# A later due time for the residual's transposes, an own due time for a projection's second half, and bias tables stored in 16 parts

## The chip, the cores and the metric

The kernel runs on one core of a Trainium2 chip. The metric is the device time of one execution in microseconds (us). TensorE is called PE, VectorE DVE, ScalarE ACT, GpSimd POOL; SP is the engine whose queue issues every DMA here.

## The reference, cut to what matters

Four layers work on a [256, 1024] float32 array. Each layer is: a half-step SwiGLU feed-forward (1024 to 2 x 2816 to 1024), a token mixer, and a second half-step feed-forward. Each of these three sub-layers has an RMS norm before and after it, and its normed output is added to the residual x.

```python
for i in range(4):
    g = norm_g[i]
    x = x + 0.5 * rms_norm(swiglu(rms_norm(x, g[0]), ffn_w_in[i, 0], ffn_w_out[i, 0]), g[1])
    m = mixer[i % 3](rms_norm(x, g[2]))       # 0: sliding window, 1: sparse, 2: block
    x = x + rms_norm(m, g[3])
    x = x + 0.5 * rms_norm(swiglu(rms_norm(x, g[4]), ffn_w_in[i, 1], ffn_w_out[i, 1]), g[5])
```

All mixers have 16 heads of 64 and add a bias to their scores that depends on the distance of query and key and on the head. Two tables hold it: table 1 with the 128-wide band for layers 0 and 3, table 0 for layers 1 and 2.

## The kernel before, in words

**Two chains.** The 256 rows are two tiles of 128, and each tile is a chain (`Chain(0)`, `Chain(1)`) that goes through all layers. A chain is a Python generator: it emits a piece of work and then yields the time at which its next piece can start. Chain 0 leads by up to a few weight slabs (`LEADS`). Weights are streamed once: SP loads half slabs of 128 x 1024 float32 into four `raw` buffers, ACT rounds each to `hi`, DVE subtracts to `lo`, and both chains multiply by both parts. An activation is also held as `xh` and `xl`, so a product takes three matmuls: hi by xh, lo by xh, hi by xl. The slots for `hi` and `lo` (28 in the pool `p4`) are shared with the tables and the mixers' arrays; `room()` counts them.

**The rough clock.** The order of PE's instructions is written out by the generators: PE runs in program order (`ORDERED`), and the framework orders the other engines. The order comes from a rough clock in the kernel's builder. `Clock.book` gives each ACT, DVE, POOL and DMA instruction a rough time, `when(tile)` says when a tile will have been written by that clock, and each yield carries such a time. `choose` takes of all generators the one whose time is earliest (not before now), and on a tie the one with the lower rank: the setup first, then chain 0, then chain 1. A yield whose second member is True also waits until the next weight slab has been split. None of this exists on the chip: a wrong rough time shows up as PE waiting in order for something late, while other work stands behind it.

**What runs at a boundary.** At the end of each sub-layer `boundary` takes the sum of squares of the accumulator (ACT), multiplies by the gain (DVE, `k<-acc,g`), takes the reciprocal root (POOL, `r`) and adds to the residual in two halves (DVE, `x<-k,r,x`). Then it yields `when(x_)`, and next it emits eight PE transposes of x (`trx`), from which ACT makes `xh` and DVE makes `xl`. There are 24 boundaries, of which the last two end the kernel without transposes.

**A projection.** `project(512)` in the mixers emits 12 matmuls over the first four blocks of 128 inputs, yields, and emits 12 over the last four. The feed-forward does the same in `ffn`, and there the second half has its own time, `when(self.xl[4])`. In `project` the yield carries 0.0: due at once.

**The mixers' core.** `core` does four heads at a time: scores on PE (`acc<-k,k`), bias on DVE (`k<-acc,bias`), exponent on ACT, transposes of the probabilities on PE (`trp`), copied by ACT and DVE (`pT`), and the product with the values (`pv`). `trq` are transposes of queries and keys. Bias tiles are read from a DRAM array `scratch` by four DMAs each.

**The setup.** It starts once, early in layer 0, with the lowest rank. It makes the two bias tables (PE `tab`, DVE copies to `rows`), then writes each to `scratch` with 32 copies: two DMAs of 16 copies for table 1 and two for table 0, with `SGAP` us of the rough clock after each. Only after the last does it give back two slots of the pool (`drop(3, 2)`).

Of the kernel before, what the change touches and what calls it, by code (L numbers as in the profile page):

```python
# [22 lines left out]
H = 16  # L23
# [10 lines left out]
LT = 384  # L34
GELU_C = 0.7978845608028654

REP = 32
# [6 lines left out]
PACE = 1.2  # L44
LATE = 6
SETUP = 30
SGAP = 8
SOON = 3
HALVES = (slice(0, DH), slice(DH, P))
FIRST, CMP_CORE = -1, 1.5  # L50
# [97 lines left out]
class Clock:  # L148
# [8 lines left out]
    def when(self, *tiles):  # L157
        return max(self.written.get(tile_of(a), 0.0) for a in tiles) + self.LAG

    def free(self, *tiles):  # L160
        return max(self.read.get(tile_of(a), 0.0) for a in tiles) + self.LAG
# [20 lines left out]
def tile_of(a):  # L182
    return getattr(a, "tensor", a).name
# [77 lines left out]
def trunk(ctx: ExitStack, tc: tile.TileContext, x, rel, gains, pre, sinks, pos, w1, w2, wts, hot,  # L261
          cmask, bmask, out, scratch):
    clock = Clock()
    when, free = clock.when, clock.free
    nc = Engines(tc.nc, clock)
# [34 lines left out]
    def k4(who, shape, dtype=F32):  # L300
        plan.held[who] += 1
        assert sum(plan.held) + 2 * (plan.split - plan.freed) <= SLOTS
        return p4.tile(shape, dtype, tag="k4", name="k4")

    def drop(who, n=1):
        plan.held[who] -= n

    def k2(shape, dtype=F32):
        return p2.tile(shape, dtype, tag="k2", name="k2")

    def bank(shape, name):
        p = mm_ps.tile(shape, F32, tag="mm", name=name)
        banks.append(p)
        if len(banks) > 4:
            clock.read[tile_of(p)] = free(banks.pop(0))
        return p

    def free_bank():
        return free(banks[0]) if len(banks) == 4 else 0.0
# [14 lines left out]
    def setup():  # L334
        relx = const.tile([33, 2, H], F32, name="relx")
        hots = k4(3, [P, HALF])[:33, :2 * LT]
        nc.sync.dma_start(relx[0:32], rel)
        nc.vector.memset(relx[32:33], 1.0)
        nc.sync.dma_start(hots, hot)
        nc.sync.dma_start(cm, cmask)  # L340
        nc.sync.dma_start(bm, bmask)
        nc.sync.dma_start(post, pos)
        nc.sync.dma_start(w2s, w2)
        for a in range(2):
            nc.sync.dma_start(nsink[:, a, :], sinks[a:a + 1, :].broadcast_to([P, H]))
        yield when(hots, relx), False
        rows = k4(3, [P, HALF])[:H, :2 * LT].rearrange("p (a b) -> p a b", a=2)
        for i in range(2):
            p = bank([P, 512], "tab")
            nc.tensor.matmul(p[:H, :LT], relx[:, i, :], hots[:, i * LT:(i + 1) * LT],  # L350
                             start=True, stop=True)
            nc.vector.tensor_copy(rows[:, i, :], p[:H, :LT])
        nc.vector.tensor_scalar_mul(nsink, nsink, -1.0)
        for i in (1, 0):
            for c in range(0, REP, REP // 2):
                nc.sync.dma_start(scratch[i, :, c:c + REP // 2],
                                  rows[:, i, :].unsqueeze(1).broadcast_to([H, REP // 2, LT]))
                yield clock.now + SGAP, False
        drop(3, 2)
        plan.want[3] = 0  # L360
# [44 lines left out]
    def load_gains(*keys):  # L405

        for i, k in keys:
            if i < DEPTH and k < 6:
                g = pg.tile([P, D], F32, tag="g", name="g")
                nc.sync.dma_start(g, gains[i, k:k + 1, :].broadcast_to([P, D]))  # L410
                gains_on[i, k] = g

    class Chain:
# [72 lines left out]
        def boundary(self, acc, this, coef, last=False):  # L486


            t = self.t
            x_ = xt[t]  # L490
            g = self.gain(*this)
            cols = [slice(q * 512, (q + 1) * 512) for q in range(2)]
            r = self.rsqrt(self.var(acc, 1.0 / (coef * coef)))
            ys = []
            for c, a in zip(cols, acc):
                y = k2([P, 512])
                nc.vector.tensor_tensor(y, a, g[:, c], op=ALU.mult)
                ys.append(y)
            accs.extend(acc)
            for c, y in zip(cols, ys):  # L500
                nc.vector.scalar_tensor_tensor(x_[:, c], y, r, x_[:, c], op0=ALU.mult, op1=ALU.add)
                if last:
                    nc.sync.dma_start(out[t * P:(t + 1) * P, c], x_[:, c])
            if last:
                return
            yield max(when(x_), free_bank()), False
            i, k = this
            norm = 6 * i + k + 1
            self.split_T(x_, 0, norm)
            self.split_T(x_, 1, norm)  # L510
            self.v = self.var([x_[:, c] for c in cols], 1.0)
            if t:
                load_gains(((norm + 1) // 6, (norm + 1) % 6))
            yield when(self.xl[0]), True
# [14 lines left out]
        def project(self, n):  # L529
            p = bank([P, 512], "proj")  # L530
            if n > 256:
                self.proj(p, n, 0, 4)
                yield 0.0, True
                self.proj(p, n, 4, 8)
            else:
                self.proj(p, n, 0, 8)
            return p
# [527 lines left out]
    with tc.manual_schedule(engines=ORDERED):  # L1065
        make_identity(tc.nc, ident)
        nc.vector.memset(mhalf, -0.5)
        for c in (slice(0, 512), slice(512, 1024)):
            nc.sync.dma_start(xt[0][:, c], x[:P, c])
        nc.sync.dma_start(pres, pre)  # L1070
        load(2)
        nc.sync.dma_start(xt[1], x[P:, :])
        for t in range(2):
            start(both[t].run(), t, t * LATE)
        n = 0
        while running:
            if n:
                feed(n < 8)
            best = choose()
            while best is None:  # L1080
                assert feed(True)
                best = choose()
            (at, _), one = best
            clock.now = max(at, clock.now)
            n += 1
            if n == SETUP:
                start(setup(), FIRST)
            got = next(one[1], None)
            if got is None:
                running.remove(one)  # L1090
            else:
                one[2:] = got
            done = min(c.at for c in both)
            plan.freed = last_half[done - 1] if done else 0
# [29 lines left out]
```

## Time and profile before

| | us |
|---|---|
| median of 3 runs | 1977.15 (1976.63 to 1980.09) |
| the profiled execution's own time | 1981.12 |
| its span, first to last instruction | 1979.3 |
| PE busy | 1938.0 (98%) |
| PE weight loads busy | 1586.7 (80%) |
| DVE busy | 1234.2 (62%) |
| ACT busy | 1039.2 (53%) |
| DMA queues, share of 16 engines | 55.7% |
| mean granted PE clock | 0.994 |

A matmul's busy time includes the pipeline, so consecutive matmuls overlap in the records and a busy PE isn't PE at its peak. What tells is the distance from one start to the next: 0.228 us for a product of 128 x 128 with 512 columns where nothing disturbs it.

### The profile page before, as it was taken

How to read it: one execution, taken by the hardware profiler on the slowest of the kernel's cores; microseconds unless marked ns; L12 is line 12 of the kernel's file. 1: busy time of each engine (PE TensorE's matmuls, PEld its weight loads, DVE VectorE, ACT ScalarE, POOL GpSimd, SP SyncE). 2: the span in 40 equal slices, each digit the busy share in tenths (PEclk: the TensorE clock that was granted, in tenths of full speed). 3: DMA queues.
4: the chain of work that ended last, by engine and by line, in shares of the span. 5: the costliest groups of instructions: out<-in, count | busy, mean ns of one | idle time of the engine just before them, and what ended most of it. 6: DMA issues, size and time to landing. Idle time of an engine off the chain costs nothing.

```text
span 1979.3 us, 27414 instructions
## 1 busy us (share of the span) xinstructions
PE 1938.0 (98%) x9978; PEld 1586.7 (80%) x9978; DVE 1234.2 (62%) x2267; ACT 1039.2 (53%) x1885; POOL 43.0 (2%) x62
## 2 busy tenths in 40 slices
PE   7999999999999998999999999999999999999998
PEld 6778878888888876788888888778888888878887
DVE  6566666556655648765576556566557655676554
ACT  6345655445544546554455455655445544665442
POOL 0000000000000000000000000000000000000000
PEclk9999999999999999999999999999999999999999
DMA  8758556555556454465556555655555555436551
GB/s 271 210 192 241 176 137 200 190 185 186 195 188 193 153 165 116 139 202 188 185 170 209 185 185 175 188 148 196 185 189 181 195 188 191 161 112 205 185 186 58
DMA packets 114131, 356.42 MB, mean 180 GB/s; under 512 B 12843, under 2 KB 30507, under 8 KB 113996
## 3 DMA queue, kind: packets, MB, share of 16 engines
q1 hardware_dynamic: 113996, 354.68, 55.4%
q8 instruction: 78, 1.28, 0.3%
q14 instruction: 57, 0.47, 0.1%
HBM read 352.01 MB, written 2.62 MB: 179 GB/s over the span
## 4 chain that ended last, share of the span: by engine, by line
PE 90%; ACT 3%; DVE 3%; DMA 2%; issue 1%; SPq 0%; POOL 0%; DVEq 0%; POOLq 0%; ACTq 0%
PE proj L228 56%; PE acc L228 29%; ACT k L210 2%; PE trh L235 2%; DVE k L210 2%; DMA raw<-wts 1%; PE trx L235 1%; DVE lo L210 1%; PE pv L228 1%; DMA bias<-scratch 1%; PE trp L235 1%; ACT hi L210 1%; DVE pT L210 0%; PE trq L235 0%; ACT xh L210 0%
## 5 line engine op out<-in xcount | busy, mean ns | idle before, releaser
L210 DVE TENSOR_TENSOR lo<-raw,hi 128x1024 fp32r<-128x1024 f32 x625 | 760.3, 1223 | 371.3 <-ACT hi L210 338.7
L210 ACT ACTIVATE hi<-raw 128x1024 fp32r<-128x1024 f32 x625 | 659.3, 1063 | 369.3 <-PE acc L228 187.5
L228 PE MATMUL proj<-hi,xh 128*128 128x512 f32 (+1 forms) x1696 | 673.9, 398 | 2.7 <-DVE xl L210 1.7
L228 PE MATMUL proj<-lo,xh 128*128 128x512 f32 (+1 forms) x1696 | 657.4, 389 | 0.8 <-DVE lo L210 0.8
L228 PE MATMUL proj<-hi,xl 128*128 128x512 f32 (+1 forms) x1696 | 448.6, 387 | 0.0
L228 PEld LDWEIGHTS proj<-hi,xh 128*128 128x128 f32 x1696 | 320.0, 189 | 64.0 <-ACT xh L210 2.8
L228 PEld LDWEIGHTS proj<-lo,xh 128*128 128x128 f32 x1696 | 320.4, 189 | 61.4 <-DVE lo L210 1.1
L228 PEld LDWEIGHTS proj<-hi,xl 128*128 128x128 f32 x1696 | 315.6, 188 | 67.3
L228 PE MATMUL acc<-hi,hh 128*128 128x512 f32 x704 | 223.7, 392 | 3.1 <-ACT hh L210 3.1
L228 PE MATMUL acc<-lo,hh 128*128 128x512 f32 x704 | 222.2, 389 | 0.0
L228 PE MATMUL acc<-hi,hl 128*128 128x512 f32 x704 | 191.3, 390 | 0.0
L210 ACT ACTIVATE h<-proj,rh 128x256 f32<-128x256 f32 x176 | 81.9, 465 | 182.3 <-PE proj L228 180.8
L210 ACT ACTIVATE hh<-trh 128x256 fp32r<-128x256 f32 x176 | 67.0, 380 | 180.8 <-PE trh L235 180.7
L228 PEld LDWEIGHTS acc<-hi,hh 128*128 128x128 f32 x704 | 130.9, 188 | 30.2 <-ACT hh L210 3.9
L228 PEld LDWEIGHTS acc<-hi,hl 128*128 128x128 f32 x704 | 132.1, 188 | 27.7
L228 PEld LDWEIGHTS acc<-lo,hh 128*128 128x128 f32 x704 | 132.1, 188 | 27.6
L210 DVE SCALAR_TENSOR_TENSOR h<-h,proj 128x256 f32<-128x256 f32 x176 | 73.6, 418 | 116.2 <-ACT h L210 116.1
L210 DVE TENSOR_TENSOR hl<-trh,hh 128x256 fp32r<-128x256 f32 x176 | 73.9, 420 | 113.2 <-ACT hh L210 113.1
L210 DVE SCALAR_TENSOR_TENSOR h<-proj,c,h 128x256 f32<-128x256 f32 x176 | 85.0, 483 | 5.1
L210 ACT ACTIVATE k<-k,nm 128x128 f32<-128x128 f32 (+1 forms) x160 | 70.7, 445 | 32.0 <-DVE nm L210 32.0
L210 POOL TENSOR_TENSOR r<-v,mhalf 128x1 f32<-128x1 f32 x48 | 36.0, 750 | 1818.4 <-DVE v L210 1818.4
L235 PE MATMUL trh<-ident,h 128*128 128x128 f32 x352 | 67.0, 272 | 0.0
(99 smaller groups left out, 1133.4 us busy)
## 6 DMA issues: line engine op xcount, KB each, us to landing
raw<-wts SPq DMA_DIRECT2D x624, 512.0 KB, 4.6
bias<-scratch SPq DMA_DIRECT2D x96, 128.0 KB, 4.6
g<-gains SPq DMA_DIRECT2D x12, 512.0 KB, 4.8
k<-w SPq DMA_DIRECT2D x8, 512.0 KB, 8.3
scratch<-k SPq DMA_DIRECT2D x4, 384.0 KB, 6.6
out<-x SPq DMA_DIRECT2D x4, 256.0 KB, 2.0
x<-x SPq DMA_DIRECT2D x2, 256.0 KB, 3.0
x<-x SPq DMA_DIRECT2D x1, 512.0 KB, 7.2
```

Of the source, the lines that this page charges most:

```text
L210: return call(out, *args, **kw)
L228: self.engine.matmul(out, lhs, rhs, **kw)
L235: self.engine.transpose(out, src, ident)
```

## The change

Four edits. `SGAP` goes from 8 to 6. The tables are stored in parts of 4 copies instead of 16: 16 DMAs in place of 4, the same bytes. At a boundary the time that is yielded for the transposes of x is 1.5 us of the rough clock later (`SLACK`). In `project` the second half is due when `xl[4]` is written by the rough clock, no longer at once.

```diff
-SGAP = 8
+SGAP = 6
+SLACK = 1.5
...
         for i in (1, 0):
-            for c in range(0, REP, REP // 2):
-                nc.sync.dma_start(scratch[i, :, c:c + REP // 2],
-                                  rows[:, i, :].unsqueeze(1).broadcast_to([H, REP // 2, LT]))
+            for c in range(0, REP, 4):
+                nc.sync.dma_start(scratch[i, :, c:c + 4],
+                                  rows[:, i, :].unsqueeze(1).broadcast_to([H, 4, LT]))
                 yield clock.now + SGAP, False
...
-            yield max(when(x_), free_bank()), False
+            yield max(when(x_) + SLACK, free_bank()), False
             i, k = this
...
                 self.proj(p, n, 0, 4)
-                yield 0.0, True
+                yield when(self.xl[4]), True
                 self.proj(p, n, 4, 8)
```

## Rows read from the trace of the kernel before

**Rows 1.** The table of busy times by stretch (busy us and count of PE, PE weight loads, DVE, ACT, POOL; then the granted clock, the DMA engines' share and GB/s): a stretch of feed-forward, and three with mixers' cores.

```profile
50.00:75.00 25.00, 25.00 (x113) 20.60 (x114) 15.85 (x21) 11.79 (x15) 0.00 (x0) 1.00 0.67 220
...
750.00:775.00 25.00, 20.27 (x302) 15.74 (x298) 23.10 (x98) 15.73 (x55) 1.56 (x2) 1.00 0.34 96
...
1275.00:1300.00 25.00, 21.89 (x243) 17.44 (x243) 18.99 (x99) 20.26 (x75) 0.00 (x0) 1.00 0.50 139
...
1725.00:1750.00 25.00, 23.21 (x175) 17.45 (x173) 17.57 (x87) 18.59 (x66) 0.00 (x0) 0.86 0.56 158
```

**Rows 2.** The waits of PE over the whole span, longest first: who waited, for whom, us in total, times, the longest.

```profile
PE trx L235 <- DMA x<-x: 8.4, 2, 4.7
...
PE trx L235 <- DVE x L210: 2.4, 2, 2.0
...
PE proj L228 <- DVE xl L210: 1.7, 2, 1.3
```

**Rows 3.** The setup's store and the bias reads: the DMA issues of the span, the instructions on the tile `scratch` and on the tile `bias` (shortest, median and longest duration, first and last start).

```profile
raw<-wts SPq DMA_DIRECT2D x624, 512.0 KB, 4.6
bias<-scratch SPq DMA_DIRECT2D x96, 128.0 KB, 4.6
...
scratch<-k SPq DMA_DIRECT2D x4, 384.0 KB, 6.6
```

```profile
L248 SPq DMA_DIRECT2D bias<-scratch x96: 302/430/1672, 146.6 to 1743.8; - x96
L248 SPq DMA_DIRECT2D scratch<-k x4: 332/384/426, 82.2 to 116.8; - x4
```

```profile
L210 DVE CUSTOM_DVE_ANT_0 k<-acc,bias x160: 254/340/425, 235.6 to 1759.8; 128x128 f32<-128x128 f32 x80, 128x256 f32<-128x256 f32 x80
```

**Rows 4.** The timeline of SP's queue around the first stores (start, us, operation, count), and the load of the DMA engines from 80 to 120 us in 40 slices of 1 us.

```profile
82.21 0.98 SPq L248 DMA_DIRECT2D scratch<-k  x2
84.90 7.72 SPq L248 DMA_DIRECT2D raw<-wts  x4
92.67 0.42 SPq L248 DMA_DIRECT2D scratch<-k  x1
104.95 1.46 SPq L248 DMA_DIRECT2D raw<-wts  x2
```

```profile
DMA  9507888888999899997000000178788961004789
GB/s 258 205 20 98 101 101 100 98 101 110 164 313 197 213 283 410 430 385 177 12 0 0 0 0 0 25 221 246 287 270 315 418 266 49 0 0 160 242 315 361
```

**Rows 5.** The timeline of ACT and of PE at 102 to 106 us.

```profile
102.24 0.47 ACT L210 ACTIVATE h<-proj,rh 128x256 f32<-128x256 f32 x1 [2.37 <-PE proj L228]
102.61 3.89 ACT L210 ACTIVATE hi<-raw 128x1024 fp32r<-128x1024 f32 x4
```

```profile
102.72 0.39 PE L228 MATMUL proj<-lo,xh 128*128 128x512 f32 x1
103.72 0.50 PE L228 MATMUL proj<-hi,xh 128*128 128x512 f32 x1 [0.60 <-ACT hi L210]
104.98 0.50 PE L228 MATMUL proj<-lo,xh 128*128 128x512 f32 x1 [0.76 <-DVE lo L210]
```

**Rows 6.** The timeline of PE at two boundaries of chain 0 at a feed-forward's end, then the transposes `trx` alone in four such boundaries' stretches (at 217.8 that of chain 1, for comparison).

```profile
198.80 1.08 PE L228 MATMUL proj<-hi,xl 128*128 128x512 f32 x4
199.97 1.23 PE L235 MATMUL trx<-ident,x 128*128 128x128 f32 x8
200.96 0.71 PE L228 MATMUL acc<-hi,hh 128*128 128x512 f32 x2
```

```profile
1692.68 1.08 PE L228 MATMUL proj<-hi,xl 128*128 128x512 f32 x4
1693.75 1.23 PE L235 MATMUL trx<-ident,x 128*128 128x128 f32 x8
1694.73 0.48 PE L228 MATMUL acc<-hi,hh 128*128 128x512 f32 x1
```

```profile
217.80:219.20 1.40, 1.03 (x8) 0.81 (x8) 0.00 (x0) 0.66 (x3) 1.00 0.88 325
657.00:658.40 1.40, 1.23 (x8) 0.84 (x8) 0.00 (x0) 0.00 (x0) 1.00 0.77 298
1008.90:1010.30 1.40, 1.23 (x8) 0.84 (x8) 0.00 (x0) 0.00 (x0) 1.00 0.79 281
```

**Rows 7.** The timeline at the end of layer 0's mixer, chain 0's boundary beside the last products of chain 1's core.

```profile
272.71 1.42 DVE L210 SCALAR_TENSOR_TENSOR x<-k,r,x 128x512 f32<-128x512 f32 x2
...
273.61 1.94 PE L235 MATMUL trx<-ident,x 128*128 128x128 f32 x8 [1.98 <-DVE x L210]
...
274.38 0.68 DVE L210 COPY pT<-trp 128x512 f32<-128x512 f32 x1
...
275.48 1.79 PE L228 MATMUL pv<-k,pT 128*64 128x64 f32 x32
...
277.20 0.50 PE L228 MATMUL proj<-hi,xh 128*128 128x512 f32 x1
```

**Rows 8.** Chain 1's boundary at the start of layer 1's mixer: the timeline of PE, then the table by stretch at and after it (columns as in rows 1).

```profile
677.29 1.05 PE L228 MATMUL proj<-hi,xl 128*128 128x48 f32 x8
...
678.18 1.09 PE L235 MATMUL trx<-ident,x 128*128 128x128 f32 x8
...
679.63 0.76 PE L228 MATMUL proj<-hi,xh 128*128 128x512 f32 x1 [0.36 <-ACT xh L210]
```

```profile
679.70:683.12 3.42, 3.42 (x8) 2.71 (x9) 3.07 (x12) 3.42 (x11) 0.35 (x1) 0.50 0.83 266
683.12:686.50 3.38, 3.38 (x16) 2.75 (x15) 3.38 (x5) 1.72 (x2) 0.19 (x1) 1.00 0.48 147
```

**Rows 9.** Chain 1's boundary at the start of layer 2's mixer, timeline.

```profile
1214.04 1.03 PE L235 MATMUL trx<-ident,x 128*128 128x128 f32 x8
...
1217.27 0.47 PE L228 MATMUL proj<-hi,xh 128*128 128x512 f32 x1 [1.31 <-DVE xl L210]
```

**Rows 10.** The table by stretch, from chain 0's boundary before a mixer to chain 1's boundary behind it, for layers 0 and 3, which run the same mixer (columns as in rows 1).

```profile
199.97:305.69 105.72, 103.12 (x702) 84.77 (x703) 72.37 (x224) 67.83 (x190) 4.20 (x6) 0.98 0.55 156
```

```profile
1693.75:1802.59 108.84, 105.64 (x703) 86.52 (x703) 72.96 (x224) 68.46 (x190) 3.29 (x6) 0.97 0.44 136
```

## The prediction

> **What bounds the kernel now.** Read the table of busy times by stretch first [rows 1]. In the feed-forward PE is busy for the whole stretch (25.00 of 25.00) with 113 matmuls, 0.22 us each, which is the undisturbed distance: nothing can be won there but work, and the change removes no matmul. The mixers' cores are the exception: 20.27, 21.89 and 23.21 of 25. So PE sets the end, and what the change can move is the sum of PE's stalls. Read next what PE waited for [rows 2]: the named waits are small, 8.4 us of the largest fall before the first matmul, and the two that the edits aim at, transposes behind x and products behind `xl`, are 2.4 and 1.7 us. These are only the waits long enough to show as idle time; shorter ones must be read as distances between starts.
>
> The sum is made against the profiled execution (span 1979.3 us, own time 1981.12 us), which is 0.2% above the median of 1977.15 us; a saving of a few us is carried over to the median as it is.
>
> **Part 1, the tables' store in 16 parts.** The first two stores go out back to back at 82.21 us, and while they move the DMA engines are 80 to 90% busy at only 98 to 110 GB/s for eight slices; the four raw halves issued at 84.90 move only from about 90 us on, at up to 430 GB/s [rows 4]. For 12 us after that SP issues nothing but one store. What follows: ACT makes four `hi` in one row at 102.61, directly behind an `h` that itself came only with the proj of 102.24, and PE, at two successive matmuls, waits for `hi` and for `lo` [rows 5]. From start to start these are 103.72 - 102.72 = 1.00 and 104.98 - 103.72 = 1.26 us against 0.228 each, so 0.77 + 1.03 = 1.80 us lost. I take the big store to be the cause; with a quarter of the bytes each and one or two block periods between them, the parts should fit between the raw loads: **-1.8 us**, bounds -1.8 and, if it isn't the cause, 0.
>
> What is added: 12 more issues on SP, 0.33 to 0.43 us each by the four seen [rows 3], about 5 us on a queue that otherwise waits for buffers: 0. The store also lasts longer. The four DMAs took 34.6 us from first to last, 11.5 us a step with a gap of 8. PE emits in chunks of 12 matmuls, 2.75 us, so a gap of 6 becomes about 8.4 us, and the sixteenth part goes out at about 82 + 15 x 8.4 = 208 us. Table 1 comes first and is complete at about 141 us; its first read now goes out at 146.6 and its first use on DVE is at 235.6 [rows 3], so even a read held back to 215 us would land (4.6 us) in time: 0. Two slots for the weights are held some 90 us longer. From 50 to 75 us they were held as well, and PE was busy for all 25.00 us [rows 1]: 0. If that cover fails, the price is a stall such as the one above, 1.8 us each.
>
> A rule speaks against this part. The Trainium skill, DMA: Bandwidth & Descriptors (Anatomy of one DMA), gives every DMA a fixed cost of about 2.0 us whatever its size, and its Rules for kernel authors ask for few large transfers; by that rule 12 more DMAs would add, as an estimate, 24 us if all of it were serial on a path that counts. In the trace a bias read of 128 KB takes as long to land as a raw half of 512 KB, 4.6 us [rows 3], so a cost that doesn't shrink with the size is there; but it is a time to landing, and weights are loaded four halves ahead. It is a rival below.
>
> **Part 2, the slack at feed-forward ends.** At chain 0's boundaries PE's order puts `trx` right where x is written. At 199.97 us the four matmuls from 198.80 should take 0.91 us and the transposes come 1.17 later: 0.26 lost; the eight transposes then take 0.99 instead of 0.79 us, the first four running ahead of the second half of x: 0.20 more. At 1693.75 it is 0.16 + 0.19 [rows 6]. At 657.0 and 1008.9 us the transposes are as long, 1.23 us busy against 1.03 at a boundary of chain 1 that doesn't wait [rows 6]. Seven boundaries are of this kind (two behind each of three layers' feed-forwards, one in the last); between 0.46 and nothing I take 0.25 each: **-1.7 us**. With the slack a chunk of chain 1 (2.75 us) goes first, and x has long been there. Chain 0 resumes 2.75 us later; chain 1's remaining chunks cover that. Bounds: -3.2 and 0.
>
> **Part 3, the slack at the start of layer 1's mixer.** `trx` at 678.18 is followed by chain 1's own projection at 679.63, which waits for the `xh` of these very transposes; 1.45 us from start to start where 0.79 would do. From 679.70 the granted clock is 0.50, the lower of its two levels (1.2 GHz), for 3.42 us, after a stretch of products with 48 columns and transposes, and only 8 matmuls fall there where the next stretch of 3.38 us, at full clock, has 16 and undisturbed 15 would start: 7 x 0.228 = 1.6 us [rows 8]. With slack, chain 0's next projection chunk comes before the transposes and breaks both. **-2.2 us**, bounds -2.3 and 0.
>
> **Part 4, the slack at mixer ends.** This one goes the other way. At 273.61 us PE waits 1.98 us for x, with `pv` of chain 1 behind [rows 7]. With slack `pv` is put first. But its second half needs a `pT` that DVE copies only after x, from 274.38 to 275.06, because DVE runs x first; so PE waits until then, `pv` ends at about 275.5, `trx` follows, and chain 0's projection some 2.3 us behind `trx`'s start (273.61 + 2.3 is well before its 277.20, which `pv` set), at 277.8 instead of 277.20: about +0.6 to 0.9 us, out_proj's transposes filling the hole. Three layers end so (0, 2, 3): +2.4 us if all orders flip; I take half, **+1.2 us**, bounds 0 and +2.7.
>
> **Part 5, the second half of a projection.** In a feed-forward nothing changes. In a mixer only the first projection behind a boundary has `xl[4]` later than now, so layers 1 and 2 are touched, twice each. The wait in layer 2 stands before the first half (1217.27, 1.31 us [rows 9]), and that half is already due by `xl[0]`: this edit doesn't reach it, nor does the slack, since x had been written over 2 us when `trx` came. I take **0**; if the other chain's chunk were put there it could be -1.3, and if it delays chain 0's queries +2.75 us, one chunk.
>
> **What can't be worked out.** Every edit shifts the order in the cores, and the stalls there depend on it. Layers 0 and 3 run the same mixer and differ by 108.84 - 105.72 = 3.1 us [rows 10]. I take that as the size by which order alone moves one mixer, either way, value 0.
>
> **Sum.** -1.8 - 1.7 - 2.2 + 1.2 = -4.5 us: 1977.15 - 4.5 = 1972.65.
>
> **The rivals.**
> - *Gains eaten up.* The stores aren't the cause of the stall at 103 us, and all mixer ends flip: -1.7 - 2.2 + 2.7 = -1.2, 1976 us. For it: nothing in the trace ties the late `hi` to the store but the order of SP. Against: the engines' low rate just then.
> - *Slower: chain 1 is late in the mixers.* Its transposes come one chunk later at each mixer's start, so its core ends 2.75 us later, at a time when chain 0 has only its out_proj and short of that nothing to fill with. Four mixers by 2.75 is +11 us: 1972.65 + 11 = 1983.6. It decides where PE idles in the last core, as at 750 to 775 us (4.7 us [rows 1]). Against it: chain 0's next feed-forward may run ahead and fill.
> - *Slower: parts in front of weights.* Each part takes its time to land in SP's order, and where a raw half behind it is late PE stalls as at 103 us. By sixteen it would be 29 us; with three, 5.4 us, and without part 1's gain: 1977.15 + 5.4 - 2.7 = 1980 us. [...] Against it: the 128 KB bias reads between raw loads from 146 us on [rows 3] left PE undisturbed.
> - *Cores gain as well.* More of chain 1's projections are left to fill chain 0's core: two mixers by 3.1 us more, 1966 us.
>
> **How the numbers follow.** About 0.2%, 4 us, is what a measurement of this kernel can tell from no change: below 1973.2 is faster, above 1981.1 slower. The forecast has 0.44 (its own range 1968 to 1977), gains eaten up 0.24, late chain 1 0.20, parts in front 0.04, cores gaining 0.08. Faster: 0.08 + about three quarters of 0.44 + 0.01 = 0.42. Slower: three quarters of 0.20, most of 0.04 and the edges of the others, 0.21. Same: 0.37. The range runs from the best rival to the worst, 1965 to 1984.
>
> **What would show it.** Part 1: no wait of PE for `hi` or `lo` between 82 and 220 us, and sixteen stores. Part 2: PE's `trx` at feed-forward ends over 1.5 us behind x and 1.03 us busy. Part 3: granted clock 1.00 around 680 us. Part 4: `pv` ahead of `trx` at the end of mixers, with a wait for `pT`. It would be wrong if the mixers' stretches changed by more than 3 us each, or if `hi` came later than PE wants in the first 220 us.

## The result, and the profile after

The change takes 1992.3 us (median of 4 runs, 1992.07 to 1992.68), the kernel before beside it 1977.72 us (4 runs). The ratio is 1.0072 with an interval of 1.0055 to 1.0090: **slower by 0.7%**, where 1972.65 us was forecast, and outside the range of 1965 to 1984 us. The profiled execution has a span of 1990.5 us and an own time of 1992.33 us, 11.2 us more than that of before in both. The medians are 14.6 us apart, because the profiled execution of before (1981.12 us) was 3.4 us above its median.

From the page of the kernel after: the span, the busy times, the shares of the chain that ended last, and the parts' row of the DMA issues (KB each, median us to landing).

```profile
span 1990.5 us, 27436 instructions
PE 1940.0 (97%) x9978; PEld 1586.7 (80%) x9978; DVE 1235.1 (62%) x2267; ACT 1038.4 (52%) x1885; POOL 34.2 (2%) x62
PE 84%; ACT 5%; DVE 5%; DMA 3%; issue 1%; POOL 0%; SPq 0%; DVEq 0%; POOLq 0%; ACTq 0%
scratch<-k SPq DMA_DIRECT2D x16, 96.0 KB, 4.8
```

Same matmuls, PE busy 2 us more in a span 11.2 us longer: the time went into waits, and PE's share of the last chain fell from 90% (the page of before) to 84%. So read next what PE waited for (us in total, times, longest).

```profile
PE proj L229 <- DVE xl L211: 5.7, 4, 2.6
PE pv L229 <- DVE pT L211: 4.9, 7, 2.1
...
PE proj L229 <- ACT xh L211: 2.6, 6, 0.5
...
PE trh L236 <- DVE h L211: 2.3, 2, 2.0
```

The same list of before has this for `pv`, and nothing for `trh`:

```profile
PE pv L228 <- DVE pT L210: 3.1, 5, 1.2
```

The wait of `trx` for x, 2.4 us in [rows 2], isn't in this list any more, as the edit meant. In its place the projection waits 5.7 us for `xl` where it was 1.7 [rows 2], `pv` waits longer for `pT`, and `trh` waits for `h`.

**Where the 11.2 us lie.** Chain 1's transposes `trx` are the same instructions in both kernels, and the difference of their starts is the lag gathered so far: 0.66 us at 217.91, 4.39 at 305.69, 6.15 at 678.18, 7.43 at 1214.04, 11.81 at 1342.13 and 11.09 at 1802.59 (times of before). Between these marks I compared PE's n-th matmul of one kernel with the n-th of the other, where their orders agree:

| place | us |
|---|---|
| first 82 us | +2.77 |
| the stall at 103 us | -1.93 |
| first feed-forward ends of layers 0 to 2 | -0.18, +0.17, +0.59 |
| end of layer 0's mixer | +3.73 |
| second feed-forward ends of layers 0 to 2 | +1.59, +1.07, +0.77 |
| start of layer 1's mixer | -4.27 |
| end of layer 1's mixer | +3.89 |
| end of layer 2's mixer | +4.40 |
| layer 3 | -1.49 |

They add to 11.1, and 0.1 comes behind the last mark. Three mixer ends alone make 12.0. Not all of the rest is the change's doing. Of the +2.77, 2.7 stand at 57 us, ahead of everything that was edited: the first part of the store goes out at 85.0 us, and PE's order first differs at 154. Near 50 us PE waits for `hh`, longer in after (second row), and then the granted clock of after is half for 3.4 us (columns as in [rows 1]), where that of before is full.

```profile
49.88 0.73 PE L228 MATMUL acc<-hi,hh 128*128 128x512 f32 x2 [2.64 <-ACT hh L210]
50.94 0.73 PE L229 MATMUL acc<-hi,hh 128*128 128x512 f32 x2 [3.17 <-ACT hh L211]
```

```profile
52.20:55.60 3.40, 3.40 (x9) 2.63 (x8) 2.05 (x4) 1.16 (x3) 0.00 (x0) 0.50 0.80 235
```

Of the -4.27, two stretches of half clock that are absent (at 680 and 707 us) give 3.2, and 1.1 comes from a third, near 775 us, which in after falls partly on a wait. In sum, half clock lasts as long in both: 20.5 us before (four stretches of 3.4 and one of 6.8), 20.5 after (six of 3.4), both without the end of the span.

**The end of layer 0's mixer**, which answers to [rows 7]. First the row of before from which distances are counted, then the timeline of after.

```profile
270.54 1.09 PE L235 MATMUL trp<-ident,k 128*128 128x128 f32 x8
```

```profile
271.21 1.09 PE L236 MATMUL trp<-ident,k 128*128 128x128 f32 x8
...
273.00 0.69 PE L229 MATMUL pv<-k,pT 128*64 128x64 f32 x16 [0.69 <-ACT pT L211]
273.38 1.42 DVE L211 SCALAR_TENSOR_TENSOR x<-k,r,x 128x512 f32<-128x512 f32 x2
...
275.05 0.68 DVE L211 COPY pT<-trp 128x512 f32<-128x512 f32 x1
...
275.78 0.69 PE L229 MATMUL pv<-k,pT 128*64 128x64 f32 x16 [2.10 <-DVE pT L211]
...
276.40 1.09 PE L236 MATMUL trx<-ident,x 128*128 128x128 f32 x8
276.52 1.06 ACT L211 ACTIVATE hi<-raw 128x1024 fp32r<-128x1024 f32 x1 [0.81 <-PE pv L229]
...
277.33 1.04 PE L236 MATMUL trx<-ident,k 128*128 128x128 f32 x8
...
277.48 2.15 ACT L211 ACTIVATE xh<-trx,pres 128x128 fp32r<-128x128 f32 x8
...
278.25 0.15 DVE L211 TENSOR_SCALAR rh<-r 128x1 f32<-128x1 f32 x1 [0.73 <-POOL r L211]
...
278.52 1.23 DVE L211 TENSOR_TENSOR lo<-raw,hi 128x1024 fp32r<-128x1024 f32 x1
...
279.67 2.15 DVE L211 SCALAR_TENSOR_TENSOR xl<-trx,pres,xh 128x128 fp32r<-128x128 f32 x8
...
280.93 0.77 PE L229 MATMUL proj<-hi,xh 128*128 128x512 f32 x1 [2.57 <-DVE xl L211]
```

Read it as two waits. The slack puts `pv` ahead of `trx`. The first half of `pv` runs on the `pT` that ACT copied; the second needs the one that DVE copies, and DVE does both halves of x first, so PE stands 2.10 us. Then come eight transposes of x and the eight of chain 1's out_proj (`trx<-ident,k`), and the projection waits 2.57 us for `xl`. It doesn't multiply by `xl`; but `bank` hands out four PSUM tiles in turn, `trx` and out_proj's transposes took all four, so that the projection's is the first of `trx`, free when the fourth `xl` has read it. The eight start 0.26 us apart and take 0.34 each, so the fourth ends at 279.67 + 3 x 0.26 + 0.34 = 280.79, and the projection starts at 280.93. And `xl` is late because on DVE `rh`, which waits 0.73 us for POOL's `r`, and then `lo` stand ahead of it, and on ACT `hi` ahead of `xh`. From `trp` to the projection it is 9.72 us, before 277.20 - 270.54 = 6.66.

**A second feed-forward's end**, timeline of PE in the kernel after.

```profile
476.85 1.03 PE L236 MATMUL trx<-ident,x 128*128 128x128 f32 x8
477.73 0.38 PE L236 MATMUL trh<-ident,h 128*128 128x128 f32 x2
...
478.63 0.50 PE L229 MATMUL proj<-hi,xh 128*128 128x512 f32 x1 [0.52 <-ACT xh L211]
...
479.83 0.50 PE L229 MATMUL proj<-hi,xh 128*128 128x512 f32 x1 [0.47 <-ACT xh L211]
```

`trx` no longer waits for x and takes its 1.03 us. But chain 1's 12 products, which before stood between `trx` (469.75) and the next projection (473.51), have gone ahead of `trx`, and the projection waits twice for `xh`.

**The end of layer 1's mixer**, timeline of after: both chains' boundaries now fall together, and on DVE chain 1's `x` and two `lo` are ahead of the `rh` that chain 0's `h` needs, and then chain 1's own `rh`, which waits 0.73 us for POOL, is ahead of `h`.

```profile
834.41 1.42 DVE L211 SCALAR_TENSOR_TENSOR x<-k,r,x 128x512 f32<-128x512 f32 x2
...
835.75 2.45 DVE L211 TENSOR_TENSOR lo<-raw,hi 128x1024 fp32r<-128x1024 f32 x2
...
838.11 0.15 DVE L211 TENSOR_SCALAR rh<-r 128x1 f32<-128x1 f32 x1
...
838.36 0.47 ACT L211 ACTIVATE h<-proj,rh 128x256 f32<-128x256 f32 x1 [0.81 <-DVE v L211]
...
839.32 0.15 DVE L211 TENSOR_SCALAR rh<-r 128x1 f32<-128x1 f32 x1 [0.73 <-POOL r L211]
...
840.38 0.44 PE L236 MATMUL trh<-ident,h 128*128 128x128 f32 x2 [2.03 <-DVE h L211]
```

### The profile page after: what moved, and what is told of

It reads as the page before. It is cut to its first block, busy times and chain, and to the rows that moved or that the text cites. A ratio compares the mean times of both kernels' runs of the same rounds, so it can differ in the third digit from the quotient of the medians.

```text
span 1990.5 us, 27436 instructions
## 1 busy us (share of the span) xinstructions
PE 1940.0 (97%) x9978; PEld 1586.7 (80%) x9978; DVE 1235.1 (62%) x2267; ACT 1038.4 (52%) x1885; POOL 34.2 (2%) x62
## 4 chain that ended last, share of the span: by engine, by line
PE 84%; ACT 5%; DVE 5%; DMA 3%; issue 1%; POOL 0%; SPq 0%; DVEq 0%; POOLq 0%; ACTq 0%
PE proj L229 54%; PE acc L229 26%; DMA raw<-wts 3%; ACT k L211 2%; PE trh L236 2%; ACT hi L211 2%; DVE k L211 2%; DVE lo L211 2%; PE trx L236 1%; ACT junk L211 1%; PE pv L229 1%; PE trp L236 1%; DVE x L211 0%; DVE pT L211 0%; POOL r L211 0%
## 5 line engine op out<-in xcount | busy, mean ns | idle before, releaser
L236 PEld LDWEIGHTS trh<-ident,h 128*128 128x128 f32 x352 | 48.3, 139 | 24.5 <-DVE h L211 2.5
```

The costliest lines, as they stand in the source:

```text
L236: self.engine.transpose(out, src, ident)
```

## The experiments

The ratio is to the kernel before on the same chip, with 95% intervals from five rounds; its medians there were 1980.6 to 1981.7 us, so only ratios are compared. Two readings of the loss are set against each other: that of the prediction's part 4 (the second `pT` behind x on DVE), and that chain 1's work, which covered chain 0's boundary, is spent too early.

The built programs show one thing without a run: the later `xl[4]` in `project` leaves every engine's instructions and their order as they were, alone and within the change. The slack at mixer ends moves PE's order only at chain 0's boundaries of layers 0, 1 and 2.

**Slack alone.** Only the later due time, at every boundary; the tables are stored as before.

```diff
-            yield max(when(x_), free_bank()), False
+            yield max(when(x_) + SLACK, free_bank()), False
```

> The kernel before with the slack at every boundary, and nothing else of the change. Theory (the slack is the whole loss, and the parts save some 2 us): 1994 us, about 16 us over before, with the same steps at the mixers' ends as the changed kernel (about +4 us each in layers 0, 1 and 2). Rival (the store in parts, which holds two slots and reads the bias later, has a share of the loss): below 1990 us.

1.0065 [1.0040, 1.0090]. The slack carries the loss.

**Parts alone.** `SGAP = 6` and parts of 4 copies.

> The kernel before with the store in 16 parts and the gap of 6, and nothing else. Theory (part 1 of the prediction): the stall of PE at 103 us is gone, 1.8 us, so about 1976 us; no new wait of PE before 225 us. Rival (the parts cost something later): 1979 us or more, with a wait for hi, lo or bias that before doesn't have.

0.9980 [0.9964, 0.9996]; PE's stall at 103 us is gone. The gap of 6 and the number of parts were not changed apart. This is the first version that beats both kernels. Its profile had an accident that bears on part 3: the table by stretch at the same place as [rows 8] (columns as there), and PE's timeline.

```profile
672.60:676.00 3.40, 3.04 (x28) 2.80 (x27) 3.30 (x6) 3.40 (x8) 0.24 (x1) 1.00 0.47 154
676.07:679.49 3.42, 3.42 (x15) 2.84 (x16) 3.06 (x12) 3.42 (x11) 0.36 (x1) 1.00 0.78 252
```

```profile
674.55 1.09 PE L236 MATMUL trx<-ident,x 128*128 128x128 f32 x8
676.00 0.50 PE L229 MATMUL proj<-hi,xh 128*128 128x512 f32 x1 [0.36 <-ACT xh L211]
```

Same products, same wait of 0.36 us, and then 15 matmuls at full clock where [rows 8] has 8 at half; PE's order here is that of before.

**Slack by kind of boundary.** The slack is multiplied by a condition; `this` holds the layer and the number of the norm behind the sub-layer that ends: with 1 the boundary is a mixer's start, with 3 its end, with 5 a second feed-forward's end.

```diff
+            yield max(when(x_) + SLACK * (this[1] == 3), free_bank()), False
```

> The slack at the boundaries behind the mixers alone (two per layer). Theory (the order at the mixers' ends, chain 1's last products put ahead of chain 0's transposes, carries the loss): +3.7 us in layer 0, +4 in layer 1, +4.4 in layer 2, together about 1989 us. Rival (the feed-forwards' ends carry it, where chain 0 stands alone behind its own transposes): 1982 us or less.

1.0068 [1.0043, 1.0092]: as much as the slack everywhere.

With `this[1] == 1`:

> The slack at the boundaries ahead of the mixers alone (two per layer). Theory (parts 2 and 3 of the prediction were right there): the stretch of half clock near 680 us and that near 707 us go, about -3 us in layer 1, and little elsewhere: 1975 us. Rival (each boundary with slack costs, wherever it stands): 1980 us or more.

0.9988 [0.9974, 1.0002], no effect that can be told; the half clock still stands at 680.0 and 707.3 us, so part 3's gain isn't there.

With `this[1] == 5`:

> The slack at the boundaries from a layer's second feed-forward to the next layer alone; of PE's order three places change, one per layer. Theory (the transposes come after chain 1's products that had covered xh): +1.4, +1.1 and +0.7 us, a wait of the projection for xh each time, 1981 us. Rival (part 2 of the prediction: the wait for x goes and nothing else comes): 1977 us.

1.0008 [0.9995, 1.0021]. The two waits for `xh` are in its trace (0.46 and 0.47 us from 474.88), and the three places make PE later by 1.54, 0.70 and 0.64 us, but the total doesn't tell it from none.

**One layer, and then its second `pT` on ACT.** Slack at the end of layer 0's mixer alone, `this == (0, 3)`, where of PE's order only chain 0's boundary moves:

> The slack at one place alone, behind layer 0's mixer; of PE's order only this place changes. Theory (cover lost: chain 1's last products no longer stand between chain 0's transposes and its projection): PE waits twice, some 2 us for pT and 2.5 us for xl, in place of 2 us once; +3 to +4 us, half a stretch of low clock either way, so 1980.5 to 1982 where before is 1977.7. Rival (the boundaries interact, one alone is cheap): +1 us or less.

1.0026 [1.0013, 1.0039]. Its timeline of PE:

```profile
269.95 1.09 PE L236 MATMUL trp<-ident,k 128*128 128x128 f32 x8
...
274.52 0.69 PE L229 MATMUL pv<-k,pT 128*64 128x64 f32 x16 [2.10 <-DVE pT L211]
275.14 1.09 PE L236 MATMUL trx<-ident,x 128*128 128x128 f32 x8
...
279.67 0.47 PE L229 MATMUL proj<-hi,xh 128*128 128x512 f32 x1 [2.57 <-DVE xl L211]
```

The same 9.72 us. Now the same order of PE, with the last `pT` of that core copied by ACT; the rough clock still books it on DVE (`end`), so that PE's order stays; ACT's and DVE's order behind it does change. With `sink == 0` it is layer 0 alone.

```diff
+                        if half and sink == 0 and t and n == len(jobs):
...
+                            tc.nc.scalar.activation(pT, p, AF.Copy)
-                        if half:
+                        elif half:
                             nc.vector.tensor_copy(pT, p)
```

> As the run before it, but the last pT of chain 1 is copied by ACT, so that it no longer stands behind x on DVE; PE's order is the same. Rival, the prediction's step (the price is pT queued behind x on DVE): the loss of the run before goes to +1 us or less. Theory (cover lost): the wait for pT turns into a wait of the transposes for x, and the wait of the projection for xl stays at 2 us or more; at least half of the loss stays.

0.9986 [0.9972, 0.9999]: the loss is gone. Timeline of PE, ACT's copy, and DVE's `xl`:

```profile
270.93 1.09 PE L236 MATMUL trp<-ident,k 128*128 128x128 f32 x8
...
272.55 0.60 ACT L733 ACTIVATE pT<-trp 128x512 f32<-128x512 f32 x1
...
272.72 1.17 PE L229 MATMUL pv<-k,pT 128*64 128x64 f32 x32 [0.69 <-ACT pT L211]
...
274.00 1.29 PE L236 MATMUL trx<-ident,x 128*128 128x128 f32 x8
...
276.23 2.15 DVE L211 SCALAR_TENSOR_TENSOR xl<-trx,pres,xh 128x128 fp32r<-128x128 f32 x8
...
277.50 0.47 PE L229 MATMUL proj<-hi,xh 128*128 128x512 f32 x1 [1.34 <-ACT junk L211]
```

From `trp` to the projection 6.57 us, so 3.15 regained: 2.12 of it before `trx` (5.19 to 3.07), where `pv` doesn't wait for DVE, and 1.03 behind it (4.53 to 3.50). Chain 1's work stands where the change put it, and the time is back all the same: for layer 0 the theory of the spent cover falls. The 1.03 has a cause that this run doesn't separate from the copy: ACT's `hi` now comes after `xh`, and DVE's `rh` after `xl`. The projection still starts when the fourth `xl` has read its tile, 276.23 + 0.78 + 0.34 = 277.35, 0.15 us ahead of it as against 0.14 in the change; the trace puts the wait down to `junk`, which the projection doesn't use.

The medians of these two runs, 1987.32 and 1979.67 us, are 7.65 apart, more than the 3.15 of the waits. The mean granted clock over the 12 executions of each is 0.9930 and 0.9960. Over the 35 executions of before on the same chip it goes from 0.991 to 0.999 and the time from 1974.0 to 1989.7 us, by a straight line 1.5 us for each 0.001; so, as an estimate, some 4.5 us of the difference goes with the clock. One stretch of half clock, at 280.0 us, is seen to go at this place; why the others come less often was not shown.

The control, the kernel before with ACT's copy in layer 0:

> Control: the kernel before, its order on PE untouched, with layer 0's last pT copied by ACT. If that copy is a gain by itself, whatever the order: -2 us or more. If it matters only where pv is put ahead of the transposes (the theory now): within 1 us of before, since pv isn't what PE waits for there.

1.0003 [0.9990, 1.0016]: without the slack the copy gains nothing.

**Layer 1's end**, `this == (1, 3)`:

> The slack at one place alone, behind layer 1's mixer. Theory (chain 1's last products come earlier, so its boundary's work on ACT and DVE falls in front of chain 0's first h, and PE waits for h): +2.2 us for that wait and up to 1.7 us of low clock, +2 to +4 us, with PE trh waiting for DVE h some 2.3 us near 840 us. Rival (that wait comes from layer 0's shift): +1 us or less and no such wait.

1.0021 [1.0007, 1.0035], by another wait; from its waits of PE:

```profile
PE trh L236 <- DVE h L211: 2.1, 1, 2.1
```

There is no `pv` in front of these transposes, and the start after it is 2.3 us later. Here the two chains do meet.

**The whole change with ACT's copy** in every layer (`half and t and n == len(jobs)`), PE's order as in the change.

> The whole change, with the last pT of chain 1 copied by ACT in every layer, PE's order untouched. Theory (the pT behind x on DVE is the price in layers 0 and 2; layer 1 and the feed-forwards' ends are others): of the 14.6 us some 7 to 8 go, 1984 to 1986 us, the waits for pT near 276 and 1320 us gone, that for h near 840 us still there. Rival (it is lost cover, and layer 0 alone was luck): at most 3 us go, 1989 us or more.

1.0011 [0.9998, 1.0023], against 1.0072 for the change: by these about 12 of the 14.6 us between the medians, more than the 7 to 8 that were expected. Against the trace of the change it is 4.73 us shorter at layer 0's end and 3.46 at layer 2's, stretches of half clock behind the waits included. Of the remaining 2.9 us between the two traces 2.1 already stand at 66 us, where no edit has acted; 1.6 more is a half clock at 840 us that doesn't come, and 1.2 is lost again to one at 1276 us. Two of its waits of PE:

```profile
PE pv L229 <- DVE pT L211: 3.0, 4, 1.2
...
PE trh L236 <- DVE h L211: 2.2, 2, 2.1
```

The 2.1 of `pv` is gone, that of `trh` stays.

**What to keep.** The change with the slack at mixer starts only, and the kernel before with parts and ACT's copy:

> The changed kernel with the slack kept only ahead of the mixers, and the store in parts. Theory (the losses all stand at the two other kinds of boundary): the 2 us of the parts and the 2 us of the mixers' starts add up, 1974 us, better than both kernels. Rival (the gain at the mixers' starts was only the luck of the clock): 1976 us.

0.9979 [0.9967, 0.9991].

> The kernel before with the store in parts and the last pT of chain 1 copied by ACT in every layer. Theory: the parts' 2 us and little more, 1975 us; if ACT is relieved of nothing and DVE of 0.68 us where x and xl queue, up to 1 us for each of three layers more: 1972 us.

0.9981 [0.9966, 0.9996]. Both are what the parts alone give; nothing adds to it. All three are 0.2% faster than the kernel before.

## Why the prediction was wrong

**Part 1 was right.** -1.8 us was forecast for the stall at 103 us; it is gone in the change, -1.93 us there, and in the parts alone. Only the pace was off: the last part goes out at 160.9 us, not 208, so the step is about 5 us and not 8.4; and the row of slow slices in [rows 4] has seven of them, not eight. The timed gain, 0.9980 [0.9964, 0.9996], is 4 us with bounds of 0.8 and 7; the trace shows 1.93 of it at the stall, and the mean granted clock, 0.996 over 12 executions against 0.995 before, goes with some of the rest. The rival of parts in front of weights fell: between 82 and 225 us PE waits for no `hi` or `lo`. The SP row of the parts in after (shortest, median and longest ns, first and last start) and the load of the DMA engines from 83 to 123 us, in 40 slices:

```profile
L249 SPq DMA_DIRECT2D scratch<-k x16: 338/426/552, 85.0 to 160.9; - x16
```

```profile
DMA  9318627785568874377475395944696853967534
GB/s 315 139 23 100 74 61 254 250 168 176 228 218 229 254 245 166 92 254 270 106 270 201 107 295 160 197 197 131 188 288 226 257 202 138 250 242 254 170 144 125
```

The long row of slices at 98 to 110 GB/s [rows 4] is gone. A part lands in 4.8 us, the whole store of four times its size took 6.6 [rows 3]. The Trainium skill, DMA: Bandwidth & Descriptors (Anatomy of one DMA), gives a fixed cost for DMAs that GpSimd issues. The prediction took that section for every DMA, and here SP issues them all. That the time to landing shrinks so little agrees with such a cost, but the 24 us that the prediction worked out for a serial path didn't come: between 82 and 225 us PE has no wait at all.

**Part 2 failed at its cover.** That `trx` would come behind a finished x was right. "Chain 1's remaining chunks cover that" was not: at a second feed-forward's end those chunks are what the slack moved ahead, and the three places cost +0.8 to +1.6 us each instead of -0.25. The first feed-forward ends of layers 0 to 2, also forecast at -0.25 each, came out at -0.18, +0.17 and +0.59.

**Part 3 was wrong.** The step "chain 0's next projection chunk comes before the transposes" didn't happen: the order at 678 us is unchanged. And the half clock there isn't tied to this wait: in the change, and in the parts alone, the same wait of 0.36 us stands at the same instructions and the clock behind it is full. Of the term's 2.2 us, 1.6 stood on one execution's clock.

**Part 4 had the mechanism and missed its size, and with it the sign.** `pv` went first and its second half waited for the `pT` behind x, as described. `trx` came 5.19 us after `trp`, forecast 4.96. The step that failed is the next: "chain 0's projection some 2.3 us behind `trx`'s start"; it was 4.53. Out_proj's transposes, said to fill the hole, take two banks and so tie the projection to `xl`, and `xl` stands behind `lo`. So one end cost 3.06 us to the projection and 3.73 by the next mark, not 0.6 to 0.9. The count was off as well: layers 0, 1 and 2 flip, not 0, 2 and 3, and layer 1 by a wait that I hadn't listed (`h` behind the other chain's boundary). Three ends: +12.0 us, half clock behind the waits included, against +1.2 in the sum. The range's bound of +2.7 rested on the same 2.3 us.

**Part 5 was right** at 0, since no order changes.

**The rivals.** "Gains eaten up" had the mixer ends flip, which they did, but at no more than 0.9 us each. "Chain 1 is late in the mixers" had the sign, and at 1983.6 us it was the nearest; but its mechanism, chain 1's core ending later with nothing to fill, isn't what the traces show. It is chain 0's projection that comes late, behind chain 1's last `pv`. "Cores gain as well" fell: the slack at mixer starts does reorder layer 3's mixer (-1.5 us by place), but alone it measures 0.9988 [0.9974, 1.0002], no gain that can be told.

**What stays open.** Layer 2's end was not run alone; its share rests on the place in the trace and on ACT's copy (3.46 us back). The slack alone and the parts alone multiply to 1.0045, and the change measures 1.0072 [1.0055, 1.0090]; the intervals overlap, no more. Layer 1's wait for `h` was shown by a run, but no run takes it away. Of the +2.77 us in the first 82 us, 0.88 is there when the last part of the input x lands (the second group of `trx` begins at 11.23 us, in the kernel before at 10.35) and 0.55 is left of it at 45; the longer wait for `hh` and the half clock behind it make the rest. With nothing edited ahead of them they are taken for scatter between executions, which one trace of each kernel can't show.

## What to carry to other kernels

Where a planner moves work ahead of a wait, price the move to the next product that depends on the moved work, with everything in order on the other engines' queues and every buffer that is taken in turn, not to the moved instruction: here the wait on x was worth 2 us, and the two waits that came in its place 4.7. Try one slack for all kinds of boundary at each kind by itself: here mixer starts measured 0.9988, second feed-forward ends 1.0008 and mixer ends 1.0068. Before pricing an edit of an order, compare the two orders: two of five parts here changed nothing or something else.

## What the runs showed of the hardware

Stretches of half clock, the lower level of 1.2 GHz, come and go at the same instructions from one trace to the next. Behind the waits of after they stand so in the table by stretch:

```profile
280.90:284.30 3.40, 3.37 (x8) 2.75 (x9) 2.50 (x12) 0.07 (x1) 0.00 (x0) 0.50 0.84 208
840.70:844.10 3.40, 3.40 (x11) 2.62 (x10) 0.43 (x1) 0.38 (x1) 0.00 (x0) 0.50 0.32 119
1325.40:1328.80 3.40, 3.40 (x10) 2.63 (x9) 2.95 (x10) 0.03 (x1) 0.00 (x0) 0.50 0.45 118
```

Each follows an idle stretch of PE of 1.6 to 2.6 us, and with 8 to 11 matmuls in 3.40 us where 15 would start it costs about 1 to 1.6 us. But the layer 0 end with slack alone has its half clock at 280.0 us behind the same 2.57 us wait, the one with ACT's copy has none at its 1.34 us, and at [rows 8] a 0.36 us wait had it in the kernel before and not in the parts alone, with the same order of PE there. One program scatters as well: the 35 executions of before on one chip have mean granted clocks from 0.991 to 0.999 and times from 1974.0 to 1989.7 us. Two profiled executions can so differ by several us: a term of that size needs timed rounds, not a trace.
